# Encoder block on one core: the rotary stage in two passes, and attention's first steps in another order

## The chip, the cores and the metric

The kernel runs on one core of a Trainium2 chip. The metric is device time in microseconds (us) of one execution. The engines are TensorE (PE; its weight loads are PEld), VectorE (DVE), ScalarE (ACT), GpSimd (POOL) and SyncE (SP). Each takes its instructions in order. In this stage SP and POOL only issue DMAs.

## The reference

One encoder block on a sequence of 1024 tokens of width 1024 in float32. One input projection gives the inputs of a Hyena mixer, queries, keys, values and the gates of the two branches. What the change touches is the attention branch between the projection and the softmax, and the point where Hyena's output meets it:

```python
z = h @ w_in[l] + b_in[l]
z_hy, q, k, v, z_g = jnp.split(z, split_at, axis=-1)
...
def rms_norm(x, g):
    xf = x.astype(F32)
    y = xf * lax.rsqrt(jnp.mean(xf * xf, axis=-1, keepdims=True) + EPS)
    return (y * g.astype(F32)).astype(x.dtype)
...
def rot(u, c, s):
    u1, u2 = u[..., :quarter], u[..., quarter:]
    return jnp.concatenate([u1 * c - u2 * s, u1 * s + u2 * c], axis=-1)
...
q = (apply_axial_rope(rms_norm(q, q_gain).astype(F32), cos, sin) * (HEAD_DIM ** -0.5)).astype(v.dtype)
k = apply_axial_rope(rms_norm(k, k_gain).astype(F32), cos, sin).astype(v.dtype)
...
s = jnp.einsum('bkgqd,bksd->bkgqs', qblk, k).astype(F32)
p = jax.nn.softmax(s, axis=-1).astype(v.dtype)
return jnp.einsum('bkgqs,bksd->bkgqd', p, v)
...
g_hy, g_at = jnp.split(jax.nn.sigmoid(z_g), N_BRANCHES, axis=-1)
x = x + gt1 * ((g_hy * y_hy + g_at * y_at) @ w_out[l])
```

There are 8 query heads and 2 key heads of 64 channels. After this stage come the output projection, a router and sixteen experts with their own weights.

## The kernel before

Matrix products are made from float32 values split in a high part (a cast on ScalarE, line L140) and a low part (a difference on VectorE, L141), with three matmuls for each product: L145, L146 and L147 of `mm3`. The block runs as a sequence of stages; a scheduler sets the order of each engine's instructions from the priority under which the code issues them and from dependencies.

**The rotary stage.** The projected queries, keys and values lie in DRAM as `zq_s`, six blocks of 128 channels by 1024 tokens: blocks 0 to 3 are the queries (two heads each), block 4 the keys, block 5 the values. `by_token(b)` loads a block into a tile `X` on SP (L673; two buffers) and turns it to tokens by rows with eight transposes on TensorE (L677). `rotated(b, i)` copies them (ScalarE, L684), squares them (ScalarE, L687), sums each head (VectorE, L689), makes the reciprocal root (`rsqrt`: the square root on ScalarE, L151, then one Newton step in five small VectorE operations, L155 to L159), scales (L692), and rotates (L694, four of L700, L701, all VectorE). `by_channel` turns the result back (TensorE, L707). The keys are cast and stored as four tiles (L724 to L730), the queries as `QT` (high half ScalarE L739, low half VectorE L740, store L742). So each block is one chain through DMA, TensorE, ScalarE, VectorE, TensorE, ScalarE, VectorE, DMA, and each has its own square root.

**The gates.** The sixteen blocks m = 18 to 33 of the projection, `win_block` with the sigmoid of L749 as evacuation, are written last but issued at the priority of the stage's start, so that their matmuls (`pM<-hT,wh` and `pM<-hT,wl`) fill TensorE while the rotary chains run. The sigmoid and the square root use different function tables of ScalarE: a row ACT_TABLE_LOAD stands ahead of each switch.

**Attention.** Its tiles take SBUF addresses that the stage before has used, so their loads on the POOL queue wait for the last user of the address: the first queries (`QT`, L773), two key tiles (`KT`, L783), the values (`Vhl`, L788). Scores of 128 queries are four matmuls (L808, L809) into one of two score buffers `pS`; VectorE takes the row maximum (L814) and ScalarE the exponential with its sum (L816), which frees the score buffer. P is turned on TensorE (L825), split (`ph` L829, `pl` L830) and multiplied by the values (L843, L844).

**Hyena's output beside it.** `hyena_out` loads Hyena's result in eight quarters (`yq`, L871, SP), splits it (`yh`, ScalarE L873; `yl`, VectorE L874), and multiplies it by `why_d` (L885) a few matmuls at a time among attention's. `adaln` (L164, L166, VectorE) adds up one row of weights of the conditioning for each of its eight steps.

## Time and profile before

| what | value |
|---|---|
| time, median of 3 runs | 2242.86 us (2242.12 to 2244.29) |
| time of the profiled execution | 2241.07 us |
| its span in the trace | 2239.3 us |
| mean granted clock of TensorE | 0.98 |
| TensorE busy | 2114.6 us, 94% of the span |
| VectorE busy | 1883.8 us, 84% |
| ScalarE busy | 1313.4 us, 59% |
| DMA | 605.38 MB, 270 GB/s over the span |

The busy shares are averages over stages that have different limits. The profiled execution has 1.8 us around its span. The granted clock is that of TensorE's throttle: 1.0 is its upper level, 2.4 GHz, and 0.5 its lower, 1.2 GHz.

### The profile page before, as it was taken

How to read it: one execution, taken by the hardware profiler on the slowest of the kernel's cores; microseconds unless marked ns; L12 is line 12 of the kernel's file. 1: busy time of each engine (PE TensorE's matmuls, PEld its weight loads, DVE VectorE, ACT ScalarE, POOL GpSimd, SP SyncE). 2: the span in 40 equal slices, each digit the busy share in tenths (PEclk: the TensorE clock that was granted, in tenths of full speed). 3: DMA queues.
4: the chain of work that ended last, by engine and by line, in shares of the span. 5: the costliest groups of instructions: out<-in, count | busy, mean ns of one | idle time of the engine just before them, and what ended most of it. 6: DMA issues, size and time to landing. Idle time of an engine off the chain costs nothing. (4 is left out here: it accounts for less than half of the span.)

```text
span 2239.3 us, 26998 instructions
## 1 busy us (share of the span) xinstructions
PE 2114.6 (94%) x10090; PEld 1683.9 (75%) x10090; DVE 1883.8 (84%) x2132; ACT 1313.4 (59%) x1445; POOL 99.5 (4%) x124
## 2 busy tenths in 40 slices
PE   5899999999589999997899999999999999999997
PEld 2677788887478887774687777777778777787876
DVE  8658899997689888644898899898998989889986
ACT  4933324325477664214577667767776767677674
POOL 0011000000000000001000000000000000000000
PEclk9999999999889999998899999999999999999999
DMA  7568755446533224666699999999999999999995
GB/s 307 195 201 263 239 174 166 145 146 216 191 114 112 78 75 145 230 227 232 260 362 355 340 374 357 367 370 370 374 354 373 368 372 366 357 371 373 379 334 185
DMA packets 157190, 605.38 MB, mean 270 GB/s; under 512 B 14466, under 2 KB 51586, under 8 KB 107780
## 3 DMA queue, kind: packets, MB, share of 16 engines
q1 hardware_dynamic: 141364, 562.77, 67.3%
q0 software_dynamic: 15696, 40.90, 7.0%
q8 instruction: 79, 1.29, 0.2%
q14 instruction: 51, 0.42, 0.1%
HBM read 538.60 MB, written 65.01 MB: 270 GB/s over the span
## 5 line engine op out<-in xcount | busy, mean ns | idle before, releaser
L1227 DVE TENSOR_TENSOR el<-raw,eh 128x2048 fp32r<-128x2048 f32 (+1 forms) x469 | 867.4, 1889 | 48.6 <-ACT eh L1226 45.6
L1226 ACT CAST eh<-raw 128x2048 fp32r<-128x2048 f32 (+1 forms) x471 | 721.0, 1594 | 22.9 <-PE pM L147 10.8
L146 PE MATMUL pM<-el,xh 128*128 128x512 f32 x1024 | 405.3, 396 | 8.2 <-DVE el L1227 7.9
L145 PE MATMUL pM<-eh,xh 128*128 128x512 f32 x1024 | 406.1, 397 | 6.9 <-ACT eh L1226 6.8
L147 PE MATMUL pM<-eh,xl 128*128 128x512 f32 x1024 | 401.5, 392 | 2.6 <-DVE xl L1287 2.6
L146 PEld LDWEIGHTS pM<-el,xh 128*128 128x128 f32 x1024 | 192.7, 188 | 62.1 <-DVE el L1227 25.6
L145 PEld LDWEIGHTS pM<-eh,xh 128*128 128x128 f32 x1024 | 192.5, 188 | 50.1 <-ACT eh L1226 10.0
L147 PEld LDWEIGHTS pM<-eh,xl 128*128 128x128 f32 x1024 | 192.7, 188 | 40.9 <-DVE xl L1287 3.1
L145 PE MATMUL pM<-hT,wh 128*128 128x512 f32 x544 | 214.2, 396 | 7.7 <-ACT z L429 5.1
L147 PE MATMUL pM<-hT,wl 128*128 128x512 f32 x544 | 214.3, 394 | 0.0
L146 PE MATMUL pM<-hT,wh 128*128 128x512 f32 x544 | 214.3, 394 | 0.0
L146 PE MATMUL py<-el,hh 128*128 128x512 f32 x512 | 205.6, 401 | 1.4 <-DVE el L1227 1.3
L145 PE MATMUL py<-eh,hh 128*128 128x512 f32 x512 | 200.8, 392 | 0.4 <-ACT hh L1329 0.4
L147 PE MATMUL py<-eh,hl 128*128 128x512 f32 x512 | 200.0, 391 | 0.3 <-DVE hl L1330 0.2
L140 ACT CAST wh<-wr 128x1024 fp32r<-128x1024 f32 (+1 forms) x58 | 54.0, 932 | 162.1 <-PE pM L146 87.4
L145 PEld LDWEIGHTS pM<-hT,wh 128*128 128x128 f32 x544 | 102.7, 189 | 29.7 <-ACT z L429 5.6
L1317 ACT ACTIVATE hd<-pM 128x512 f32<-128x512 f32 x64 | 38.4, 599 | 142.2 <-PE pM L147 142.2
L146 PEld LDWEIGHTS pM<-hT,wh 128*128 128x128 f32 x544 | 102.9, 189 | 21.1 <-DVE hT L373 0.4
L147 PEld LDWEIGHTS pM<-hT,wl 128*128 128x128 f32 x544 | 102.8, 189 | 20.7
L146 PEld LDWEIGHTS py<-el,hh 128*128 128x128 f32 x512 | 96.1, 188 | 24.6 <-DVE el L1227 5.4
L145 PEld LDWEIGHTS py<-eh,hh 128*128 128x128 f32 x512 | 96.1, 188 | 22.3 <-ACT hh L1329 1.8
L147 PEld LDWEIGHTS py<-eh,hl 128*128 128x128 f32 x512 | 96.3, 188 | 19.3 <-DVE hl L1330 0.9
(380 smaller groups left out, 3399.0 us busy)
## 6 DMA issues: line engine op xcount, KB each, us to landing
raw<-in_wg_dram SPq DMA_DIRECT2D x128, 1024.0 KB, 7.2
raw<-in_wu_dram SPq DMA_DIRECT2D x128, 1024.0 KB, 7.2
raw<-in_wd_dram SPq DMA_DIRECT2D x128, 1024.0 KB, 7.7
wr<-in_win_dram SPq DMA_DIRECT2D x34, 512.0 KB, 4.1
dc<-in_dfc_dram POOLq DMA_DIRECT2D x48, 256.0 KB, 3.7
wr<-in_wada_dram SPq DMA_DIRECT2D x24, 512.0 KB, 3.7
st<-in_wada_dram SPq DMA_DIRECT2D x16, 512.0 KB, 10.0
k_s<-f SPq DMA_DIRECT2D x16, 512.0 KB, 2.8
```

The costliest lines, as they stand in the source:

```text
L140: nc.scalar.copy(h, raw)
L145: mm(o, a[0], b[0], start=start, stop=False)
L146: mm(o, a[0], b[1], start=False, stop=False)
L147: mm(o, a[1], b[0], start=False, stop=stop)
L1226: nc.scalar.copy(h[:, ks], raw[:, ks])
L1227: low = eng.tensor_sub(l[:, ks], raw[:, ks], h[:, ks])
L1317: nc.scalar.activation(hd, ps2[0], AF.Silu)
```

## The change

It has three parts.

First, the rotary stage is in two passes. `by_heads` does the loads, transposes, copies, squares and sums of all five blocks, one after the other; a single Newton chain with one square root then works on all their sums ([128 x 80] instead of five times [128 x 16]); and `rotated` does the rest, block by block. The loads (`load_z`) are issued two blocks ahead. The squares and the rotation's products lie in tiles of another pool (`zt`), the rotated block in the buffers of `X`, which are free by then.

Second, attention: the casts and differences of Hyena's output stand behind the fourth exponential and the fifth maximum (`behind` orders instructions of one engine without a semaphore), and the rows of `adaln` behind the sixth maximum.

Third, the first P tile is taken early from its pool, so that it, and not the first queries' tile, lies on the addresses which are used last in the rotary stage.

The lines of after.py are numbered a little higher than those of before: L147 becomes L152, L677 L688, L684 L700, L687 L702, L707 L724, L739 L767, L808 L838, L816 L846, L873 L903.

```diff
@@ -129,6 +129,11 @@
         tc.add_manual_dep(late.ins, early.ins.name, mybir.DependencyInfo(
             mybir.DependencyClass.Sync, mybir.DependencyReason.DATA), reason="wait")
 
+    def behind(late, early):
+
+        tc.add_manual_dep(late.ins, early.ins.name, mybir.DependencyInfo(
+            mybir.DependencyClass.NoSync, mybir.DependencyReason.DATA), reason="behind")
+
     def wload(src, cols_=1024):
         t = ring.tile([128, cols_], F32, name="wr", tag="wr", bufs=2)
         nc.sync.dma_start(t, src)
@@ -161,9 +166,9 @@
     def adaln(acc, w, k):
 
         if k == 0:
-            nc.vector.tensor_scalar(acc, w, siluc[:, 0:1], None, op0=ALU.mult)
+            return nc.vector.tensor_scalar(acc, w, siluc[:, 0:1], None, op0=ALU.mult)
         else:
-            nc.vector.scalar_tensor_tensor(acc, w, siluc[:, k:k + 1], acc, op0=ALU.mult, op1=ALU.add)
+            return nc.vector.scalar_tensor_tensor(acc, w, siluc[:, k:k + 1], acc, op0=ALU.mult, op1=ALU.add)
 
     def mod_cols(acc, g, psum):
         ps = psum([128, 8])
@@ -658,7 +663,7 @@
         tabs = []
         for i in range(2):
             g = gain[:, i]
-            tab = f4([128, 2, 8, 64])
+            tab = w2("H", [128, 2, 8, 64])
             nc.vector.tensor_mul(tab[:, 0], rope[:, 0], g[:, None, :].to_broadcast([128, 8, 64]))
             for u in range(2):
                 for h in range(2):
@@ -668,9 +673,15 @@
                                          g[:, None, i_].to_broadcast([128, 8, 16]))
             tabs.append(tab)
 
+        zs = {}
+
+        def load_z(b):
+
+            zs[b] = w2("X", [128, 1024])
+            nc.sync.dma_start(zs[b], zq_s[b])
+
         def by_token(b):
-            z = w2("X", [128, 1024])
-            nc.sync.dma_start(z, zq_s[b])
+            z = zs[b]
             for hf in range(2):
                 ps = pT()
                 for j in range(4):
@@ -678,27 +689,33 @@
                                         z[:, (hf * 4 + j) * 128:(hf * 4 + j + 1) * 128], ident)
                 yield hf, ps.rearrange("p (q c) -> p q c", q=4)
 
-        def rotated(b, i):
-            tok = f4([128, 8, 2, 64])
+        blocks = (4, 0, 1, 2, 3)
+        ms = w2("wf").rearrange("p (i n) -> p i n", i=4)[:, 0:3, 0:80]
+        toks = {}
+
+        def by_heads(n, b):
+
+            tok = toks[b] = f4([128, 8, 2, 64])
             for hf, ps in by_token(b):
                 nc.scalar.copy(tok[:, hf * 4:hf * 4 + 4].rearrange("p q h c -> p q (h c)"), ps)
+            sq = zt().rearrange("p (n c) -> p n c", n=16)
+            nc.scalar.activation(sq, tok.rearrange("p q h c -> p (q h) c"), AF.Square)
+            nc.vector.reduce_sum(ms[:, 0, n * 16:n * 16 + 16], sq, axis=AX.X)
+
+        def rotated(n, b, i):
+            tok = toks.pop(b)
             t2 = tok.rearrange("p q h c -> p (q h) c")
-            sq = f4([128, 16, 64])
-            nc.scalar.activation(sq, t2, AF.Square)
-            m = w2("ms", [128, 3, 16])
-            nc.vector.reduce_sum(m[:, 0], sq, axis=AX.X)
-            nc.vector.tensor_scalar(m[:, 0], m[:, 0], 1.0 / 64, EPS, op0=ALU.mult, op1=ALU.add)
-            rsqrt(m[:, 1], m[:, 0], m[:, 2])
-            nc.vector.tensor_mul(t2, t2, m[:, 1][:, :, None].to_broadcast([128, 16, 64]))
-            A = f4([128, 8, 2, 64])
+            nc.vector.tensor_mul(t2, t2, ms[:, 1, n * 16:n * 16 + 16][:, :, None].to_broadcast([128, 16, 64]))
+            A = w2("X", [128, 8, 2, 64])
             nc.vector.tensor_mul(A, tok, tabs[i][:, 0][:, :, None, :].to_broadcast([128, 8, 2, 64]))
+            turn = zt().rearrange("p (q h c) -> p q h c", q=8, h=2)
             for h in range(2):
                 src = tok[:, :, h].rearrange("p q (a u c) -> p q a u c", a=2, u=2)
-                dst = sq.rearrange("p (q h) c -> p q h c", h=2)[:, :, h].rearrange("p q (a u c) -> p q a u c", a=2, u=2)
+                dst = turn[:, :, h].rearrange("p q (a u c) -> p q a u c", a=2, u=2)
                 tab = tabs[i][:, 1].rearrange("p q (a u c) -> p q a u c", a=2, u=2)
                 for u in range(2):
                     nc.vector.tensor_mul(dst[:, :, :, u], src[:, :, :, 1 - u], tab[:, :, :, u])
-            nc.vector.tensor_add(A, A, sq.rearrange("p (q h) c -> p q h c", h=2))
+            nc.vector.tensor_add(A, A, turn)
             return A
 
         def by_channel(R, hf):
@@ -708,15 +725,26 @@
                                     R[:, hf * 4 + j].rearrange("p h c -> p (h c)"), ident)
             return ps
 
-        Vhl = f4([128, 2, 4, 2, 64], F32R), f4([128, 2, 4, 2, 64], F32R)
+        load_z(5)
+        load_z(4)
+        Vhl = [z4([128, 2, 4, 2, 64], F32R) for hf in range(2)]
         for hf, ps in by_token(5):
-            p4 = ps.rearrange("p q (h c) -> p h q c", h=2)
+            if hf:
+                load_z(0)
+            p4 = ps.rearrange("p q (h c) -> p h q c", c=64)
             nc.scalar.copy(Vhl[hf][:, :, :, 0], p4)
             nc.vector.tensor_sub(Vhl[hf][:, :, :, 1], p4, Vhl[hf][:, :, :, 0])
+        for n, b in enumerate(blocks):
+            by_heads(n, b)
+            if n < 3:
+                load_z(blocks[n + 2])
+        for hf in range(2):
             nc.sync.dma_start(V_s[:, hf], Vhl[hf].rearrange("p h q s c -> p (h q s c)").bitcast(F32))
+        nc.vector.tensor_scalar(ms[:, 0], ms[:, 0], 1.0 / 64, EPS, op0=ALU.mult, op1=ALU.add)
+        rsqrt(ms[:, 1], ms[:, 0], ms[:, 2])
         lo, hi = slice(0, 64), slice(64, 128)
         K = [[f4([128, 1024], F32R) for h in range(2)] for i in range(2)]
-        R = rotated(4, 1)
+        R = rotated(0, 4, 1)
         for hf in range(2):
             sl = slice(hf * 512, hf * 512 + 512)
             ps = by_channel(R, hf)
@@ -730,7 +758,7 @@
                 nc.sync.dma_start(KT_s[i, h], K[i][h].bitcast(F32))
 
         for b_ in range(4):
-            R = rotated(b_, 0)
+            R = rotated(b_ + 1, b_, 0)
             QT = [wk.tile([128, 1024], F32R, name="QT", tag="Z", bufs=4) for h in range(2)]
             for hf in range(2):
                 sl = slice(hf * 512, hf * 512 + 512)
@@ -768,6 +796,8 @@
         def w(name, shape, dt=F32, bufs=2):
             return at.tile(list(shape), dt, name=name, tag=name, bufs=bufs)
 
+        firstP = w("P", [128, 1024], bufs=6)
+
         def query(h):
             t = w("QT", [128, 1024], F32R)
             return t, nc.gpsimd.dma_start(t, QT_s[h])
@@ -776,7 +806,7 @@
         KT = [[w(f"KT{i}{h}", [128, 1024], F32R, 1) for h in range(2)] for i in range(2)]
         Vhl = w("Vhl", [128, 2, 2, 4, 128], F32R, 1)
 
-        exps = []
+        exps, maxima = [], []
 
         def keys(kv):
             for i in range(2):
@@ -811,8 +841,8 @@
                         yield
                 Sf = S.rearrange("p n k -> p (n k)")
                 c = (i % 2) * 2 + j
-                nc.vector.tensor_reduce(rs[:, c:c + 1], Sf, axis=AX.X, op=ALU.max, negate=True)
-                P = w("P", [128, 1024], bufs=6)
+                maxima.append(nc.vector.tensor_reduce(rs[:, c:c + 1], Sf, axis=AX.X, op=ALU.max, negate=True))
+                P = w("P", [128, 1024], bufs=6) if exps else firstP
                 exps.append(nc.scalar.activation(P, Sf, AF.Exp, bias=rs[:, c:c + 1], accum_out=rs[:, 4 + c:5 + c]))
                 Ps.append(P)
                 yield
@@ -870,8 +900,8 @@
                 t = yp.tile([128, 4, 128], F32, name="yq", tag="yq", bufs=2)
                 nc.sync.dma_start(t, y_s[q])
                 sl = slice(q * 128, q * 128 + 128)
-                nc.scalar.copy(yh[:, :, sl], t)
-                nc.vector.tensor_sub(yl[:, :, sl], t, yh[:, :, sl])
+                behind(nc.scalar.copy(yh[:, :, sl], t), exps[3])
+                behind(nc.vector.tensor_sub(yl[:, :, sl], t, yh[:, :, sl]), maxima[4])
             acc = yp.tile([128, 1024], F32, name="acc")
             for m in range(8):
                 raw = wload(why_d[m], 512)
@@ -890,7 +920,7 @@
                     nc.vector.tensor_mul(g, ps, g)
                     nc.sync.dma_start(m1_s[m][:, sl], g)
                     yield
-                adaln(acc, wload(wada_d[2, m]), m)
+                behind(adaln(acc, wload(wada_d[2, m]), m), maxima[5])
             mod_cols(acc, 2, pT)
 
         units = [(h, i) for h in range(8) for i in range(4)]
```

On TensorE, among the gate matmuls behind the transposes of the values and keys, the order before has only gate matmuls for more than fifty rows. In the change, the transposes of blocks 0 to 3 (L688) stand there; these are the rows around those of blocks 1 and 2:

```order
L151 MATMUL pM<-hT_340,wh 128x512
L152 MATMUL pM<-hT_332,wl 128x512
L150 MATMUL pM<-hT_333,wh 128x512
L688 MATMUL pT<-ident,X 128x128 x8
L151 MATMUL pM<-hT_341,wh 128x512
L152 MATMUL pM<-hT_333,wl 128x512
L688 MATMUL pT<-ident,X 128x128 x8
L150 MATMUL pM<-hT_334,wh 128x512
L151 MATMUL pM<-hT_342,wh 128x512
L152 MATMUL pM<-hT_334,wl 128x512
```

Two gate matmuls lie between block 1 and block 2. Block 0 stands ten gate matmuls ahead of block 1, and block 3 fourteen behind block 2.

The end of the gates on TensorE before (L146, L147 are gate matmuls; L707 are the transposes of blocks 2 and 3, rotated; L677 those of block 3's z; L808 and L809 the first scores):

```order
L145 MATMUL pM<-hT_338,wh 128x512
L146 MATMUL pM<-hT_346,wh 128x512
L147 MATMUL pM<-hT_338,wl 128x512
L707 MATMUL pT<-ident,f_3736 128x128 x8
L677 MATMUL pT<-ident,X 128x128 x8
L707 MATMUL pT<-ident,f_3792 128x128 x8
L808 MATMUL pS<-KT_4835,QT 128x512 x2
L809 MATMUL pS<-KT_4837,QT 128x512
```

and in the change (L151, L152 the gates, L724 the rotated block 3, L838 and L839 the scores):

```order
L150 MATMUL pM<-hT_338,wh 128x512
L151 MATMUL pM<-hT_346,wh 128x512
L152 MATMUL pM<-hT_338,wl 128x512
L724 MATMUL pT<-ident,X 128x128 x8
L838 MATMUL pS<-KT_4809,QT 128x512 x2
L839 MATMUL pS<-KT_4811,QT 128x512
L838 MATMUL pS<-KT_4809,QT 128x512
```

Behind the last gate matmul one group of eight transposes is left of three.

On ScalarE, the end of the rotary stage and attention's start before: the last two blocks' casts (L739), copies, square and square root of block 3 (L684, L687, L151), the casts of Hyena's output (L873), the exponentials (L816) and the high parts of P (L829):

```order
L739 CAST QT<-pT 64x512 x4
L684 COPY f_3765<-pT 128x512 x2
L687 ACTIVATE f_3780<-f_3765 128x1024
L151 ACT_TABLE_LOAD
L151 ACTIVATE ms<-ms 128x16
L739 CAST QT<-pT 64x512 x4
L873 CAST yh<-yq 128x4x128 x4
L816 ACT_TABLE_LOAD
L816 ACTIVATE P,rs<-pS,rs 128x1024 x2
L873 CAST yh<-yq 128x4x128 x2
L829 CAST ph<-pM 128x512 x2
```

and in the change (L767 the casts, L777 the sigmoid of a gate, L846 the exponentials, L859 the high parts, L903 Hyena's casts):

```order
L777 ACTIVATE ge<-pM,cols 128x512
L767 CAST QT<-pT 64x512 x4
L846 ACT_TABLE_LOAD
L846 ACTIVATE P,rs<-pS,rs 128x1024 x2
L859 CAST ph<-pM 128x512
L846 ACTIVATE P,rs<-pS,rs 128x1024
L859 CAST ph<-pM 128x512 x2
L846 ACTIVATE P,rs<-pS,rs 128x1024
L903 CAST yh<-yq 128x4x128
L859 CAST ph<-pM 128x512
L903 CAST yh<-yq 128x4x128
```

The exponentials' table load stands right behind the last block's casts, four exponentials precede the first cast of Hyena's output, and no square root is left there.

## Rows read from the trace of the kernel before

**Rows 1.** The page, part 2: busy tenths of DMA in 40 slices

```profile
DMA  7568755446533224666699999999999999999995
```

**Rows 2.** Windows: length, busy by engine, granted PE clock, DMA share, GB/s

```profile
521.00:584.00 63.00, 62.12 (x303) 49.92 (x302) 42.53 (x78) 39.68 (x55) 0.00 (x0) 1.00 0.56 201
584.00:625.50 41.50, 8.65 (x34) 6.27 (x33) 25.65 (x40) 14.83 (x24) 2.12 (x4) 0.63 0.59 212
625.50:680.00 54.50, 54.44 (x347) 47.70 (x348) 48.88 (x67) 40.92 (x73) 2.12 (x4) 0.97 0.30 100
```

**Rows 3.** Timeline of TensorE: start, us, operation, count, [idle before <-releaser]

```profile
583.70 0.39 PE L147 MATMUL pM<-hT,wl 128*128 128x512 f32 x1
589.82 1.94 PE L707 MATMUL pT<-ident,f 128*128 128x128 f32 x8 [5.73 <-DVE f L701]
...
605.65 1.94 PE L707 MATMUL pT<-ident,f 128*128 128x128 f32 x8 [9.80 <-DVE f L701]
...
609.91 0.50 PE L809 MATMUL pS<-KT,QT 128*128 128x512 f32 x1 [1.22 <-DMA KT<-KT_s]
...
625.49 0.79 PE L808 MATMUL pS<-KT,QT 128*128 128x512 f32 x1 [13.95 <-ACT P L816]
```

**Rows 4.** Timeline of ScalarE in the same stretch

```profile
616.03 1.36 ACT L873 CAST yh<-yq 128x512 fp32r<-128x512 f32 x2 [6.49 <-DMA yq<-y_s]
...
622.23 1.28 ACT L816 ACT_TABLE_LOAD   x1
```

**Rows 5.** Timeline of VectorE in the same stretch

```profile
610.30 0.75 DVE L164 TENSOR_SCALAR acc<-wr,siluc 128x1024 f32<-128x1024 f32 x1
611.09 1.28 DVE L166 SCALAR_TENSOR_TENSOR acc<-wr,siluc,acc 128x1024 f32<-128x1024 f32 x1
...
622.97 2.35 DVE L814 TENSOR_REDUCE rs<-pS 128x1 f32<-128x1024 f32 x2
```

**Rows 6.** Timeline of POOL: issues of attention's first loads

```profile
602.25 0.53 POOL L773 DMA_DIRECT2D QT<-QT_s  x1 [95.81 <-DVE f L692]
602.77 1.07 POOL L783 DMA_DIRECT2D KT<-KT_s  x2
```

**Rows 7.** Timeline of SP: issues of the loads of blocks 0 and 1

```profile
523.24 0.32 SPq L673 DMA_DIRECT2D X<-zq_s  x1
...
525.35 0.52 SPq L673 DMA_DIRECT2D X<-zq_s  x1
```

**Rows 8.** Tile X, in 523.2:523.3 and in 525.2:525.5: landing in us

```profile
DMA to landing us min/median/max: 5.2/5.2/5.2
...
DMA to landing us min/median/max: 7.3/7.3/7.3
```

**Rows 9.** Timeline of TensorE among the gate matmuls

```profile
524.72 0.60 PE L677 MATMUL pT<-ident,X 128*128 128x128 f32 x4
525.07 0.48 PE L147 MATMUL pM<-hT,wl 128*128 128x512 f32 x1
...
536.98 0.39 PE L145 MATMUL pM<-hT,wh 128*128 128x512 f32 x1
```

**Rows 10.** Timeline of VectorE: block 3's rotation, first and last, low halves

```profile
600.43 1.22 DVE L692 TENSOR_TENSOR f<-f,ms 128x1024 f32<-128x1024 f32 x1
...
604.28 1.22 DVE L701 TENSOR_TENSOR f<-f,f 128x1024 f32<-128x1024 f32 x1
...
608.24 2.02 DVE L740 TENSOR_TENSOR QT<-pT,QT 64x512 fp32r<-64x512 f32 x3 [0.17 <-ACT QT L739]
```

**Rows 11.** Timeline of TensorE in a later stage, a wait for VectorE

```profile
894.86 0.50 PE L145 MATMUL pS<-oT,wh 128*128 128x512 f32 x1 [1.60 <-DVE g L947]
```

**Rows 12.** Windows, right behind that wait

```profile
897.00:898.80 1.80, 1.80 (x5) 1.35 (x5) 0.68 (x2) 0.00 (x0) 0.00 (x0) 0.50 0.95 327
```

**Rows 13.** Lines, 521 to 626 us: loads of ScalarE's tables

```profile
L151 ACT ACT_TABLE_LOAD x5 | 6.4, 1283 | 0.1
...
L749 ACT ACT_TABLE_LOAD x4 | 5.1, 1283 | 0.1
```

## The prediction

> **What bounds the kernel now.** The page's DMA slices [rows 1] stand at nine tenths only in the second half of the span, where the experts' weights are read; the rotary stage lies near slice 10, where DMA is no limit. So I read the stretches around it [rows 2]. From 521 to 584 us TensorE is busy 62.12 of 63 us: gate matmuls bound it. From 584 to 625.5 it is busy 8.65 of 41.5, at a mean granted clock of 0.63. From 625.5 on attention keeps it busy 54.44 of 54.5, with DVE at 48.88. The hole between the two full stretches is the stage to read.
>
> TensorE's timeline there [rows 3]: the last gate matmul starts at 583.70 and ends at 584.09; the transposes of block 2's rotated queries wait 5.73 for DVE, those of block 3's 9.80; scores start, wait 1.22 for a key tile, and go on from 609.91 until both score buffers are full. Then TensorE waits 13.95 for the first exponential, until 625.49. That last wait is explained on ScalarE [rows 4]: it stands at 616.03 in a cast of Hyena's output that waited 6.49 for a DMA, and loads the exponential's table only at 622.23. On VectorE [rows 5] two adaLN rows, then the low halves of the casts, stand ahead of the first maximum, which starts at 622.97 although the matmuls of its scores began at 609.91 at the latest. The loads of attention's first tiles sat on the POOL queue until 602.25 behind a wait of 95.81 on the last block's norm [rows 6]. So 584.09 to 625.49, 41.40 us, is one chain: two blocks' rotary work one after the other, loads, then a queue of casts.
>
> **Term 1: the gates end later.** All five blocks' z transposes now stand among the first sixty gate matmuls, so TensorE, which works in order, waits in the gates where z isn't there. The loads of blocks 0 and 1 go out at 523.24 and 525.35 [rows 7], when blocks 5 and 4 are transposed; this order hasn't changed. They landed after 5.2 and 7.3 us [rows 8], at 528.4 and 532.65. Gate matmuls come every 0.229 us (52 of them from 525.07 to 536.98 [rows 9]). Block 0's transposes stand seven gate matmuls behind 525.07, so at 526.7: a wait of 1.8. Eight transposes take about 0.85. Ten gate matmuls on, at 531.6, block 1: a wait of 1.05. The load of block 2 starts when block 0 is transposed, at 529.4; landing in 5.6, an estimate nearer to the shorter of the two, it is there at 535.0, and TensorE two gate matmuls behind block 1 at 533.9: 1.1. Block 3's load starts at 533.5, lands at 539.1, and TensorE comes there at 539.0: 0.1. Sum 4.05; with landings at 5.2 throughout about 3, at 7.3 about 7.
>
> Two groups of eight transposes that stood behind the gates (block 3's z, block 2's rotated queries [rows 3]) now lie ahead of the last gate matmul: 2 x 0.85 = 1.7. The 0.85 is an estimate: four transposes at 524.72 held the next matmul off for 0.35 [rows 9], twice that is 0.70, and the matmuls around them start a little late. The 1.94 for eight in [rows 3], behind a long wait, bounds it from above. Will a rotated block be late for its transposes? A rotation takes DVE from 600.43 to 605.50, 5.07 us, and the low halves of its casts 2.02 for three of four [rows 10], 2.7 in all; with about 1 us for a weight's low half that is 8.8 per block, against 36 to 40 gate matmuls and eight transposes, 9.1 to 10.0, on TensorE. DVE just keeps up; I take 0.5 in sum, bounds 0 and 3. The norms' own chain, five squares and sums and one square root, ends near 548 and its first block is due near 556: covered by 65 gate matmuls (14.9 us); without that cover it would cost its 3 to 4 us.
>
> The clock: behind a wait of 1.60 at 894.86 [rows 11] the granted clock is 0.50, which is 1.2 GHz, up to 898.8, and five matmuls stand there in 1.8 us [rows 12] where eight would at 0.229. From 894.86 to 898.8 are 3.9 us; at half speed they lose up to 2.0, and I count 1.6 for a drop. Block 0's wait of 1.8 is of that size; most of what it costs is taken from the next two waits, since those end when a load lands. I take 1.0, bounds 0 and 4.8 (three drops). [...]
>
> Term 1 is 4.05 + 1.7 + 0.5 + 1.0 = 7.25: gates end near 591.35 instead of 584.09.
>
> **Term 2: from the gates' end to the first exponential.** The queries' tile leaves the address range whose last user was block 3's norm. By the order of the new code, its load waits for one of the last gate matmuls, and the first key load for the very last. So they go out at 591.4. Meanwhile block 3, rotated near 593, is transposed (1.94 in [rows 3]) and cast, and ScalarE loads the exponential's table (1.28 [rows 4]); with four casts of some 0.6 that is done by 597, ahead of the first maximum near 599.5. From the first key load's issue (602.77 [rows 6]) to the matmul that used the last key tile (609.91) it took 7.14; the first block of scores needs about 1.0 more; from the first maximum's start (622.97) to TensorE's restart it took 2.52. Sum 10.7: restart at 602.05, that is 23.4 us earlier than 625.49. Hyena's casts no longer lie between. The bounds of the 7.14: the two landings of [rows 8] lie 2.1 apart, so plus or minus 1.
>
> **Term 3: attention's first part.** What was done in the hole must now be done beside TensorE's work: adaLN's first three rows (0.75 + 2 x 1.28), and Hyena's casts, of which four and their low halves lay in the hole. DVE had 5.6 of 54.5 us free [rows 2]. The new load is some 2.0 for two adaLN rows and 2.8 for four low halves (0.69 each), 4.8 in all, less 1.2 since a third maximum is done before: it fits by a margin of 2. Since queues in order don't fill perfectly I take a loss of 1.5, bounds 0 and 5. Everything behind 680 keeps its order and shifts.
>
> **Sum.** 7.25 + 10.7 = 17.95 for 41.40, less 1.5: 21.95 us gained. The profiled execution took 2241.07 us (span 2239.3); it would become 2219.1. The median of the runs shown is 1.79 above it, so the forecast is 2220.9. Differences under 0.2% (4.5 us) can't be told from no change.
>
> **The rivals.**
> A: the norm pass holds TensorE longer. Landings of 7.3 (7 instead of 4.05) and three clock drops (4.8 instead of 1.0) make term 1 14.0; restart 6.75 later: 2227.7. For it: DMA is busy there, with stores of V and gate outputs beside the loads; against it: a slower TensorE arrives later at the next load.
> B: VectorE becomes the bound in early attention, by the 88 to 90% that it is already busy [rows 2]: loss 5 to 6 instead of 1.5, 2225.4. Against it: the low halves wait behind the fifth maximum, and the first use of them comes late.
> C: only the table loads count, because some other wait holds the scores where they were. Five loads for square roots and four back to the sigmoid [rows 13] become one and one: 7 x 1.283 = 9.0, so 2233.9. The Trainium skill, "ScalarE: Activation LUTs", section "What ACT_TABLE_LOAD costs", puts a switch at about 2.66 us with a drain; by that figure this case alone would be 18.6 us, an estimate. Here the load is 1.283 and nothing in the rows shows a drain of that size.
> D: no change: the gain is given back in the experts' stage, where DMA is at nine tenths [rows 1]. Against it: its buffers come free with the work ahead, so its stream shifts too. 2242.9.
> E: slower: the gate matmuls stand in order behind the z transposes. Block 3's load starts when block 1 is transposed, so when landings T are long, block 3's transposes come at about 527.9 + 2T (539.1 at 5.6, term 1), and 193 gate matmuls and the key loads stand behind them. The gain of 21.95 is gone when 2T has grown by as much, at T of 16.6, and from there every us of landing costs two: at T of 20 it would be 2249.7. Against it: of the two landings shown the longer is 7.3 [rows 8]. For it: all four loads fall into a stretch in which stores of V and of gate outputs are due.
>
> **How the numbers follow.** Forecast 0.70, with its own range 2215.9 to 2227.8 (below, all terms at their low bounds: waits -1.05, clock -1.0, rotations -0.5, keys -1, attention -1.5, together 5.05; above, half of what the upper bounds add: waits 2.95, clock 3.8, rotations 2.5, keys 1, attention 3.5, together 13.75). A 0.12, B 0.07, C 0.04, D 0.03, E 0.04. The range for 8 in 10 is 2215 to 2231: A and B and three quarters of the sum of the upper bounds lie below its upper end, C, D and E above it. Faster: 0.70 + 0.12 + 0.07 + 0.04 = 0.93; same 0.03; slower 0.04.
>
> **What would show it.** Right: four short waits of TensorE for X between 526 and 541; the last gate matmul near 591; one table load for the root, one back; key loads on POOL within 1 us of the last gate matmul; first exponential ending near 602, with no Hyena cast ahead of it; attention's end near 836 instead of 858. Wrong: gates ending after 596; waits of TensorE for rotated blocks of over 1 us each; the key load waiting for something else; TensorE waiting for `pl` or for `yl` in the first 50 us of attention; a longer gap between attention and experts than before.

## The result and the profile after

The changed kernel takes 2217.76 us (median of 4 runs, 2216.80 to 2220.59) against 2242.49 for the kernel before (4 runs): the ratio is 0.9893, with a 95% interval of 0.9876 to 0.991. That is 24.7 us less, where 21.95 were forecast. The profiled execution took 2217.21 us with a span of 2215.4, that is 23.9 under the one of before.

The windows of the changed kernel, with the columns of [rows 2]:

```profile
521.00:591.00 70.00, 64.17 (x319) 51.58 (x317) 53.28 (x78) 37.81 (x57) 2.12 (x4) 1.00 0.55 197
591.00:602.00 11.00, 6.36 (x14) 4.06 (x15) 4.73 (x7) 4.88 (x8) 0.54 (x1) 0.52 1.05 390
602.00:657.00 55.00, 53.68 (x343) 46.31 (x342) 51.54 (x72) 41.42 (x75) 1.59 (x3) 0.97 0.44 144
```

The windows are cut where the forecast put the gates' end (591.35); the gates themselves end at 587.78. From there to TensorE's restart it takes 11.99 us, where it took 41.40, and the gates' stretch is 4.70 longer (table below). From 591 to 602 the DMA engines have a share of 1.05 and move 390 GB/s; the granted clock is 0.52 there and 1.00 up to 591.

TensorE's timeline answers to [rows 3]:

```profile
528.15 1.06 PE L688 MATMUL pT<-ident,X 128*128 128x128 f32 x8 [1.54 <-DMA X<-zq_s]
...
533.84 1.06 PE L688 MATMUL pT<-ident,X 128*128 128x128 f32 x8 [0.98 <-DMA X<-zq_s]
...
564.23 1.06 PE L724 MATMUL pT<-ident,X 128*128 128x128 f32 x8 [0.50 <-DVE X L718]
...
573.00 1.06 PE L724 MATMUL pT<-ident,X 128*128 128x128 f32 x8 [0.20 <-DVE X L718]
...
587.39 0.39 PE L152 MATMUL pM<-hT,wl 128*128 128x512 f32 x1
589.26 1.06 PE L724 MATMUL pT<-ident,X 128*128 128x128 f32 x8 [1.48 <-DVE X L718]
593.78 1.19 PE L838 MATMUL pS<-KT,QT 128*128 128x512 f32 x2 [3.46 <-DMA KT<-KT_s]
595.57 0.80 PE L839 MATMUL pS<-KT,QT 128*128 128x512 f32 x1 [0.59 <-DMA KT<-KT_s]
...
599.77 0.79 PE L838 MATMUL pS<-KT,QT 128*128 128x512 f32 x1 [1.27 <-ACT P L846]
```

Two z loads are waited for, 1.54 and 0.98; two rotated blocks, 0.50 and 0.20; the last gate matmul starts at 587.39. Of the three groups of transposes behind it one is left, with a wait of 1.48. Then the key tiles are waited for, 3.46 and 0.59, and the wait for the first exponential is 1.27 where it was 13.95. TensorE restarts at 599.77 instead of 625.49.

ScalarE, VectorE and POOL answer to [rows 4 to 6]:

```profile
592.49 1.28 ACT L846 ACT_TABLE_LOAD   x1
598.51 1.11 ACT L846 ACTIVATE P<-pS,rs 128x1024 f32<-128x1024 f32 x1 [4.74 <-DVE rs L844]
```

```profile
590.58 2.63 DVE L768 TENSOR_TENSOR QT<-pT,QT 64x512 fp32r<-64x512 f32 x4 [0.86 <-ACT QT L767]
597.25 2.50 DVE L844 TENSOR_REDUCE rs<-pS 128x1 f32<-128x1024 f32 x2 [4.04 <-PE pS L839]
```

```profile
587.40 0.53 POOL L803 DMA_DIRECT2D QT<-QT_s  x1 [81.96 <-DMA QT_s<-QT]
588.08 1.06 POOL L813 DMA_DIRECT2D KT<-KT_s  x2
```

Neither a cast of Hyena's output nor an adaLN row stands between block 3's last casts and the first maximum; ScalarE waits 4.74 and VectorE 4.04 for scores, which wait for the key loads, and these go out right behind the last gate matmul.

The span can be cut at five starts that every kernel here has: block 5's first transposes, the last gate matmul, the first exponential, the last matmul with V, the first expert matmul. All are read from the timelines. The first exponential of the kernel before, which [rows 4] do not show, is this row:

```profile
624.23 1.11 ACT L816 ACTIVATE P<-pS,rs 128x1024 f32<-128x1024 f32 x1 [0.71 <-DVE rs L814]
```

| stretch | before | changed | difference |
|---|---|---|---|
| up to block 5's transposes | 521.42 | 520.41 | -1.01 |
| to the last gate matmul | 62.28 | 66.98 | +4.70 |
| to the first exponential | 40.53 | 11.12 | -29.41 |
| to attention's last matmul with V | 242.04 | 244.40 | +2.36 |
| to the first expert matmul | 212.90 | 212.23 | -0.67 |
| to the end | 1160.13 | 1160.26 | +0.13 |

The first row isn't the change's: the difference is there already at VectorE's first instruction that is not the same, a row of the rotation's table (517.50 before, 516.49 in the changed kernel), and over the other traces of this study the row goes from 520.20 to 524.56. So a profiled span is read here by its stretches. The experts' stage keeps its length to 0.13: nothing is given back there.

### The profile page after: what moved, and what is told of

Its sections match the earlier page's. It is cut to its first block, busy times and chain, and to the rows that moved or that the text cites. A ratio compares the mean times of both kernels' runs of the same rounds, so it can differ in the third digit from the quotient of the medians.

```text
span 2215.4 us, 26961 instructions
## 1 busy us (share of the span) xinstructions
PE 2113.6 (95%) x10090; PEld 1681.6 (76%) x10090; DVE 1878.2 (85%) x2108; ACT 1301.8 (59%) x1434; POOL 99.5 (4%) x124
## 5 line engine op out<-in xcount | busy, mean ns | idle before, releaser
L1256 ACT CAST eh<-raw 128x2048 fp32r<-128x2048 f32 (+1 forms) x471 | 720.9, 1594 | 23.1 <-PE pM L152 10.7
L151 PE MATMUL pM<-el,xh 128*128 128x512 f32 x1024 | 405.3, 396 | 8.1 <-DVE el L1257 7.9
L152 PE MATMUL pM<-eh,xl 128*128 128x512 f32 x1024 | 401.8, 393 | 2.7 <-DVE xl L1317 2.7
L151 PEld LDWEIGHTS pM<-el,xh 128*128 128x128 f32 x1024 | 192.7, 188 | 62.3 <-DVE el L1257 25.1
L152 PEld LDWEIGHTS pM<-eh,xl 128*128 128x128 f32 x1024 | 192.7, 188 | 40.8 <-DVE xl L1317 3.2
L152 PE MATMUL pM<-hT,wl 128*128 128x512 f32 x544 | 214.2, 394 | 0.0
L151 PE MATMUL pM<-hT,wh 128*128 128x512 f32 x544 | 214.1, 394 | 0.0
L151 PE MATMUL py<-el,hh 128*128 128x512 f32 x512 | 205.6, 402 | 1.4 <-DVE el L1257 1.3
L152 PE MATMUL py<-eh,hl 128*128 128x512 f32 x512 | 200.1, 391 | 0.3 <-DVE hl L1360 0.2
L151 PEld LDWEIGHTS pM<-hT,wh 128*128 128x128 f32 x544 | 102.9, 189 | 20.9 <-DVE hT L378 0.6
L152 PEld LDWEIGHTS pM<-hT,wl 128*128 128x128 f32 x544 | 102.8, 189 | 20.8
L151 PEld LDWEIGHTS py<-el,hh 128*128 128x128 f32 x512 | 96.1, 188 | 24.6 <-DVE el L1257 5.4
L152 PEld LDWEIGHTS py<-eh,hl 128*128 128x128 f32 x512 | 96.3, 188 | 19.3 <-DVE hl L1360 0.9
```

The source lines that it names most:

```text
L151: mm(o, a[0], b[1], start=False, stop=False)
L152: mm(o, a[1], b[0], start=False, stop=stop)
L1256: nc.scalar.copy(h[:, ks], raw[:, ks])
```

## Experiments

### Each half alone

The first kernel has the new rotary stage only, the second the new order of attention's start only.

```diff
 # two passes only
-        firstP = w("P", [128, 1024], bufs=6)
...
-                behind(nc.scalar.copy(yh[:, :, sl], t), exps[3])
-                behind(nc.vector.tensor_sub(yl[:, :, sl], t, yh[:, :, sl]), maxima[4])
+                nc.scalar.copy(yh[:, :, sl], t)
+                nc.vector.tensor_sub(yl[:, :, sl], t, yh[:, :, sl])
...
-                behind(adaln(acc, wload(wada_d[2, m]), m), maxima[5])
+                adaln(acc, wload(wada_d[2, m]), m)
```

> Only the rotary stage is changed (two passes, one root). Hyena's casts and the adaLN rows stand ahead of the first exponential as before, and the first P tile is taken where it was. If the casts ahead of the exponential are worth what their place in the old chain says, the first four casts end near 604, the exponential's table is loaded near 605, and TensorE restarts near 608 instead of 599.8 in the changed kernel; about 2 us come back in early attention, which then has less to do: 2224, some 18 under the kernel before. Rival: the loads for Hyena's casts start so much earlier that the casts are done before the scores anyway: then it equals the changed kernel, 2217.8.

> Only the order of attention's start is changed; the rotary stage is that of before. Scores start at 609.9 as before; the first maximum should follow near 611 instead of 622.97 and TensorE restart near 613.6 instead of 625.49, 11.9 earlier; early attention gives back about 2: 2232.8, some 9.7 under before. Rival: it gains all of 11.9 or more (what is lost in early attention then comes from something else than the moved casts), 2230.6; or nothing, if the casts only move the wait.

Two passes alone: 2232.38 us, ratio 0.9957 (0.9941 to 0.9974). The order alone: 2228.27 us, ratio 0.9944 (0.9926 to 0.9962). Both moved the way that was expected; the first is 8 us slower than I expected and the second 4.5 faster. (The first kernel's profiled execution was the quickest of its four, 2228.51, so its stretches flatter it.) ScalarE with two passes only:

```profile
602.50 0.62 ACT L901 CAST yh<-yq 128x512 fp32r<-128x512 f32 x1 [9.06 <-DMA yq<-y_s]
...
608.51 0.62 ACT L901 CAST yh<-yq 128x512 fp32r<-128x512 f32 x1 [1.47 <-DMA yq<-y_s]
609.14 1.28 ACT L844 ACT_TABLE_LOAD   x1
611.14 1.11 ACT L844 ACTIVATE P<-pS,rs 128x1024 f32<-128x1024 f32 x1 [0.71 <-DVE rs L842]
```

The last gate matmul starts at 587.99 there and the first exponential 23.15 later, against 11.12 in the changed kernel and 40.53 before. The casts wait 9.06 for Hyena's loads, since these go out behind the last queries' store and land in the full DMA queue (410 GB/s from 593.5 to 602.5): I had taken 604 for the fourth cast, it ends at 609.13. The order alone leaves the gates where they were (62.25 us) and brings the first exponential to 27.86 behind the last gate matmul, 12.67 sooner than before:

```profile
606.66 1.94 PE L712 MATMUL pT<-ident,f 128*128 128x128 f32 x8 [9.81 <-DVE f L706]
...
613.82 0.50 PE L813 MATMUL pS<-KT,QT 128*128 128x512 f32 x1 [2.41 <-ACT P L821]
```

The wait of 9.81 for block 3's rotation is as in [rows 3], and the one for the first exponential falls from 13.95 to 2.41. From the first exponential to attention's end it takes 242.10, against 242.04 before: the 2 us that I expected early attention to give back did not come, which was the rival of that expectation. Against the 2241.83 of the kernel before, measured beside them, the two halves are worth 9.5 and 13.6 us, 23.0 in sum, and the whole change 24.7: they take different parts of one chain.

### Which of the moved work held the scores

```diff
-                behind(adaln(acc, wload(wada_d[2, m]), m), maxima[5])
+                adaln(acc, wload(wada_d[2, m]), m)
```

> The changed kernel with adaLN's rows free to be placed as before: three rows then stand ahead of the first maximum on VectorE (0.75 + 2 x 1.28 = 3.3 us). VectorE has 4.04 us idle there in the changed kernel. Theory A: the rows wait for their weights (the first load is issued at 589.7 and takes 5, the next two follow in a ring of two buffers that Hyena's output weights share), so the first exponential comes 3 to 8 us later and most of it is lost: 2220 to 2225. Theory B: they fit into the idle time, the first exponential moves by under 1, and early attention gains the 3.3 us of VectorE: 2216 to 2217.

2233.55 us, ratio 0.9957 (0.9941 to 0.9974): theory A, and more than it said. VectorE:

```profile
598.27 0.75 DVE L169 TENSOR_SCALAR acc<-wr,siluc 128x1024 f32<-128x1024 f32 x1
604.78 1.28 DVE L171 SCALAR_TENSOR_TENSOR acc<-wr,siluc,acc 128x1024 f32<-128x1024 f32 x1 [5.76 <-DMA wr<-in_wada_dram]
611.74 1.29 DVE L171 SCALAR_TENSOR_TENSOR acc<-wr,siluc,acc 128x1024 f32<-128x1024 f32 x1 [5.67 <-DMA wr<-in_wada_dram]
613.05 2.36 DVE L844 TENSOR_REDUCE rs<-pS 128x1 f32<-128x1024 f32 x2
```

Each of the second and third rows waits nearly 6 us for its weights, and the first maximum stands behind them in order. The first exponential comes 21.88 behind the last gate matmul, close to the 23.15 of the kernel with two passes only, in which the casts stand ahead of it, with two adaLN rows, and the third part of the change is missing. So there are two queues side by side, ScalarE's casts and VectorE's adaLN rows, and either one can hold the scores. Moving the casts and not the rows brings the first exponential 1.3 us sooner, and no shorter time (2233.55 against 2232.38). Moving the rows and not the casts was not tried.

### One root, or five

```diff
             nc.vector.reduce_sum(ms[:, 0, n * 16:n * 16 + 16], sq, axis=AX.X)
+            m = ms[:, :, n * 16:n * 16 + 16]
+            nc.vector.tensor_scalar(m[:, 0], m[:, 0], 1.0 / 64, EPS, op0=ALU.mult, op1=ALU.add)
+            rsqrt(m[:, 1], m[:, 0], m[:, 2])
...
-        nc.vector.tensor_scalar(ms[:, 0], ms[:, 0], 1.0 / 64, EPS, op0=ALU.mult, op1=ALU.add)
-        rsqrt(ms[:, 1], ms[:, 0], ms[:, 2])
```

> The changed kernel with a square root and Newton chain for each block in the first pass, so eight table loads more on ScalarE, 10.3 us. My theory: they lie beside the gate matmuls and cost 0 to 3, say 1: 2218.8. Rival: one root is what the gain is made of, and it costs 8 to 10: 2226 to 2228.

2221.83 us, ratio 0.9911 (0.9894 to 0.9927); the interval overlaps the changed kernel's. The table loads are there (lines view, 521 to 600 us):

```profile
L156 ACT ACT_TABLE_LOAD x5 | 6.4, 1283 | 0.1
L778 ACT ACT_TABLE_LOAD x5 | 6.4, 1283 | 0.1
```

These are ten where the changed kernel has two, 10.3 us more on ScalarE, and the gates end 67.51 behind block 5 instead of 66.98: 0.5 (block 3's rotated transposes stand four gate matmuls ahead of the last one there, and not behind it). Another 1.6 stands between gates and first exponential, where the key tiles landed after 7.0 and 8.5 instead of 6.9. So the number of roots is not what the gain is made of. That the norms of all blocks being ready before the rotations makes it is argued from the order; no kernel here takes that away alone.

### Where the loads wait

Three kernels vary the loads between gates and scores: without the early P tile; with V's load behind the first maximum; and with attention's pools in another order, so that the first loads no longer wait for the gates.

```diff
 # loads off the gates' addresses
+        opool = right.enter_context(tc.tile_pool(name="op", bufs=1, side="right", reuse_waits="tile"))
         at = right.enter_context(tc.tile_pool(name="at", bufs=1, side="right", reuse_waits="tile"))
...
-        firstP = w("P", [128, 1024], bufs=6)
-        KT = [[w(f"KT{i}{h}", [128, 1024], F32R, 1) for h in range(2)] for i in range(2)]
+        KT = [[w("KT00", [128, 1024], F32R, 1), w("KT01", [128, 1024], F32R, 1)]]
+        late = w("KT11", [128, 1024], F32R, 1)
+        KT.append([w("KT10", [128, 1024], F32R, 1), late])
 # V late
-        nc.gpsimd.dma_start(Vhl.rearrange("p f h q c -> p f (h q c)"), V_s)
+                if len(exps) == 1:
+                    load = nc.gpsimd.dma_start(Vhl.rearrange("p f h q c -> p f (h q c)"), V_s)
+                    wait(load, maxima[0])
```

> The changed kernel without its third part: the first P tile is taken when it is first written. By the addresses, the queries' load then waits for the first and not the seventh of the last gate group's eight tiles, and the key loads for the third and fifth instead of the last. My theory: key loads go out 3 to 4 us earlier, scores start right behind block 3's transposes near 590.4 instead of 593.8, restart of TensorE 3 us earlier: 2214.8. Rival: the third part is needed, the queries' tile waits for something later than the gates and the restart comes later: 2219 or more.

> The changed kernel with the load of V (1 MB) put behind the first maximum, so that it isn't in flight beside the queries' and keys' tiles. My theory: the stretch from the gates' end to the first maximum is bound by DMA bandwidth (390 GB/s at a share of 1.0 from 588 to 600), so without V the last key tile lands about 1.5 us sooner after its issue (6.0 instead of 7.5) and the first exponential comes 1 to 1.5 us sooner behind the last gate matmul (10 instead of 11.1); V itself lands near 605, when its first matmul is due, and may cost 0 to 2 there: 2216 to 2219, no difference in the time. Rival: a fixed landing time of some 7 us whatever else is in flight; then the exponential stays at 11.1 and the kernel loses what V's landing adds, 2219 to 2221.

> The changed kernel with attention's tiles laid out otherwise (the output tiles' pool first, then the queries, the keys of the first half, V; the first P tile where it is first written): by the addresses, the first loads of queries, keys and V no longer wait for any gate matmul, only for their own stores and for users that end before 535. My theory: they go out before 580, are there when the gates end, TensorE goes from block 3's transposes to the scores without a wait near 590.4, the first maximum follows block 3's last low half near 593.3, the first exponential near 594.4 instead of 598.5, TensorE restarts near 595.6, and its clock is back sooner: 4 to 5 us under the changed kernel, 2213. Rival: the restart is bound by block 3's own chain (casts, table load) and by DMA for other tiles, and it gains 0 to 2: 2216 to 2218.

Without the early P tile: 2219.53 us, ratio 0.9898 (0.9882 to 0.9915), which can't be told from the changed kernel. The key loads do go out sooner, 2.5 and 1.1 us ahead of the last gate matmul at 589.73 instead of 0.7 and more behind it:

```profile
587.22 0.53 POOL L811 DMA_DIRECT2D KT<-KT_s  x1 [2.02 <-PE pM L152]
588.59 0.53 POOL L811 DMA_DIRECT2D KT<-KT_s  x1 [0.84 <-ACT QT L767]
```

But they land 7.4 and 8.2 us after their issue instead of 6.9, and the first exponential comes 10.04 behind the last gate matmul instead of 11.12: 1.1 of the 3 that I expected. The restart, at 601.03, finds the clock back at its upper level:

```profile
601.00:606.20 5.20, 5.13 (x29) 4.14 (x30) 3.91 (x6) 4.31 (x8) 0.53 (x1) 1.00 1.06 412
```

From the first exponential to attention's end it takes 242.49 here, 1.9 less than in the changed kernel, and attention ends 2.6 us sooner behind block 5. The next stretch, to the experts, is 2.1 longer (214.37). Whether the third part gains or costs anything can't be told from these times.

With V late: 2222.81 us, ratio 0.9912 (0.9895 to 0.9928). From 588 to 600 the DMA engines move 331 GB/s, against 356 in the changed kernel (not 390, as the expectation has it). The keys land after 5.8 and 7.2, at best a little sooner, and the first exponential stays at 11.35 behind the gates. V takes 8.3 us and is then waited for:

```profile
609.85 0.55 PE L875 MATMUL pT<-ph,Vhl 128*128 128x256 f32 x1 [2.76 <-DMA Vhl<-V_s]
```

So the landing of the keys is not V's doing alone. What else is in flight there are stores of queries and the loads for Hyena's output; that these are enough was not tested. The expectation for V's own landing (605) was too early.

With the loads off the gates' addresses:

```profile
572.43 0.53 POOL L801 DMA_DIRECT2D QT<-QT_s  x1 [66.02 <-DVE zt L717]
572.95 1.07 POOL L813 DMA_DIRECT2D KT<-KT_s  x2
```

```profile
590.79 1.06 PE L724 MATMUL pT<-ident,X 128*128 128x128 f32 x8 [1.48 <-DVE X L718]
591.61 0.71 PE L838 MATMUL pS<-KT,QT 128*128 128x512 f32 x2
...
597.30 0.80 PE L838 MATMUL pS<-KT,QT 128*128 128x512 f32 x1 [3.60 <-ACT P L846]
```

The queries' load now waits for a rotation product (`zt`) on VectorE, and the keys go out behind it, 16 us ahead of the gates' end; they land after 5.6 to 6.3, and the scores follow block 3's transposes without a wait. The first exponential comes 7.11 behind the last gate matmul, 4.0 sooner than in the changed kernel, as expected. Yet the time is 2218.15 us, ratio 0.989 (0.9874 to 0.9907), the same as the changed kernel's. The stretches say where it went: 245.20 instead of 244.40 to attention's end, 213.95 instead of 212.23 to the experts, 1162.01 instead of 1160.26 to the end. Attention still ends 2.6 us sooner behind block 5 than in the changed kernel. The stretch to the experts varies from 211.80 to 214.37 us over the kernels of this study, so its 1.72 tells nothing. The last stretch is 1160.04 to 1160.74 in all the others, also in the kernel below that has these same loads with the idle time filled, so the layout is not the cause of its 1.75. In this trace alone the clock falls once among the experts:

```profile
1227.60:1231.00 3.40, 3.40 (x8) 2.72 (x9) 3.40 (x3) 3.40 (x3) 0.00 (x0) 0.50 1.01 402
```

Half of 3.4 us is 1.7, which accounts for the 1.75. The wait ahead of that drop is on the experts' weights' casts (0.96 at 1226.89), far from the loads that this kernel moves.

### What early attention loses

TensorE's clock behind the restart, in the changed kernel:

```profile
528.10:532.00 3.90, 3.85 (x24) 3.40 (x25) 0.99 (x1) 2.71 (x4) 0.00 (x0) 1.00 0.59 174
599.70:604.90 5.20, 5.13 (x16) 4.25 (x17) 1.97 (x3) 3.17 (x7) 0.54 (x1) 0.50 1.06 404
605.00:609.90 4.90, 4.90 (x35) 4.25 (x34) 4.58 (x7) 3.86 (x8) 0.00 (x0) 1.00 0.51 181
```

For 5.2 us behind the restart the clock is at 0.50. Two kernels fill TensorE's wait with 32 transposes of a tile that is there, into a PSUM tile that nobody reads: the changed kernel behind block 3's transposes, and the kernel with the loads off the gates' addresses behind its first eight score matmuls.

```diff
+        idle = pM()
+        for n in range(32):
+            nc.tensor.transpose(idle[:, n % 4 * 128:n % 4 * 128 + 128], R[:, n % 8].rearrange("p h c -> p (h c)"), ident)
```

> The changed kernel with 32 more transposes of block 3's rotated tile on TensorE behind block 3's own, into a score-sized PSUM tile that nobody reads: work without use, which fills the wait for the key tiles (3.46 us in the changed kernel, 32 at about 0.1). Theory clock: what early attention lost there (244.4 us from the first exponential to attention's end against 242.0 before) is the lowered clock behind that wait, 0.50 for the 5.2 us behind the restart; with TensorE kept busy the scores run at 1.0, the first exponential comes about 1 us sooner behind the last gate matmul (10.1 instead of 11.1) and the stretch from it to attention's end is 242 to 242.5: 2214.6. Theory casts: the loss is Hyena's casts and adaLN beside the exponentials; then the stretch stays at 244 to 245 and the time at 2217 to 2218.

> The kernel with the loads off the gates' addresses, and 32 transposes of a key tile that nobody reads behind the first eight score matmuls, to fill the 3.60 us wait for the first exponential. Theory clock: the stretch from the first exponential to attention's end falls from 245.2 to about 242.5, since the restart is at full clock, and the kernel from 2218.2 to 2215.6. Theory casts: no difference.

In the changed kernel the filling moved the wait instead of taking it away: the scores run at full clock, the first exponential comes 10.09 behind the last gate matmul as expected, but then TensorE waits 1.86 for it, and behind that wait the clock falls after all:

```profile
591.45 3.66 PE L783 MATMUL pM<-ident,X 128*128 128x128 f32 x32
...
600.05 0.70 PE L841 MATMUL pS<-KT,QT 128*128 128x512 f32 x1 [1.86 <-ACT P L849]
```

```profile
600.20:603.60 3.40, 3.40 (x11) 2.77 (x12) 1.22 (x1) 1.40 (x3) 0.53 (x1) 0.50 1.02 411
```

From the first exponential to attention's end it took 243.90 instead of 244.40, and the time is 2218.94 us, ratio 0.99 (0.9883 to 0.9916): no gain. In the other kernel no wait is left:

```profile
593.20:597.00 3.80, 3.69 (x34) 3.43 (x32) 3.59 (x4) 3.05 (x5) 0.00 (x0) 1.00 0.98 365
597.00:602.60 5.60, 5.52 (x33) 4.54 (x34) 4.31 (x6) 4.62 (x8) 0.53 (x1) 1.00 0.99 346
```

The clock stays at 1.00, the stretch is 243.49 instead of 245.20, and the time 2216.03 us, ratio 0.9885 (0.9868 to 0.9901), 2.1 under its own base where 2.6 were expected. It is the quickest kernel here, but its interval overlaps those of its base and of the changed kernel. So in these traces the clock at the restart is worth 1.7 us of attention; the kernel without the early P tile, with its clock up and 1.9 less, agrees. The difference of the times is not clear of the noise. It can't be all of the 2.36 that attention lost, since the kernel before restarts at a lowered clock as well.

The last kernel leaves out the low halves of Hyena's output.

```diff
-                behind(nc.vector.tensor_sub(yl[:, :, sl], t, yh[:, :, sl]), maxima[4])
...
-                        for i, (a, b) in enumerate(((wh, yh), (wh, yl), (wl, yh))):
+                        for i, (a, b) in enumerate(((wh, yh), (wh, yh), (wl, yh))):
```

> The changed kernel without the low halves of Hyena's output (eight differences of 0.69 on VectorE left out; the matmuls that used them read the high halves, as many as before). Theory: what early attention still loses beside the clock is VectorE's share of the moved casts: the stretch from the first exponential to attention's end falls from 244.4 to 242 to 243 and the time to 2216. Rival: it is ScalarE's casts, or the order on TensorE; then it stays at 244 and 2217.8.

2218.55 us, ratio 0.9893 (0.9877 to 0.991), and 245.20 in the stretch: no gain, so VectorE's 5.5 us of low halves don't set it alone. TensorE waits 1.07 for a cast there:

```profile
614.09 0.74 PE L913 MATMUL pT<-yh,wh 128*128 128x512 f32 x2 [1.07 <-ACT yh L902]
```

## Why the prediction was right

**Term 1**, gates later by 7.25: measured 4.70. The waits for z are two, of 2.52 in sum, in place of four of 4.05. Block 0's load ended TensorE's wait 5.9 us after its issue; those of blocks 1 to 3 landed in 4.5 to 5.5 us, where 7.3 and 5.6 were taken, and block 1, with 1.05 forecast, was not waited for. One of the two V stores, which had been in flight beside block 1's load, goes out later now. The waits for rotated blocks are 0.70 (0.5 forecast). With 1.7 for the two groups of transposes that makes 4.9. The clock term, 1.0, measured nothing in this execution: behind the wait of 1.54 the granted clock is 1.00 (528.1 to 532.0 above). It wasn't without reason, though. In the kernel with V late, whose rotary stage is the same, the wait for block 0 happened to be 2.21, and there it fell:

```profile
526.00:530.10 4.10, 1.94 (x10) 1.29 (x8) 1.22 (x1) 1.65 (x2) 0.00 (x0) 1.00 0.93 290
530.10:534.00 3.90, 3.85 (x15) 3.30 (x16) 0.87 (x1) 2.81 (x4) 0.00 (x0) 0.60 0.64 185
```

The next z wait, 0.98 in the changed kernel, was gone there, as the prediction argued: the later loads take part of a drop up. Its net cost can't be read here: the gates ended 67.62 behind block 5, and 66.76 to 67.87 in the kernels with the same rotary stage and no drop. In the kernel with adaLN's rows free the same wait was 2.25, and the clock stayed up:

```profile
532.30 1.06 PE L688 MATMUL pT<-ident,X 128*128 128x128 f32 x8 [2.25 <-DMA X<-zq_s]
```

```profile
532.30:536.20 3.90, 3.90 (x25) 3.42 (x26) 1.03 (x1) 2.76 (x5) 0.00 (x0) 1.00 0.72 175
```

So the length of a wait alone does not say whether the clock falls. The wait of 1.60 in [rows 11], on which this term was priced, says the same: it is 1.41 in the changed kernel and 1.58 with two passes only, and the clock stays at 1.00 behind both. The drop of the kernel before, worth up to 1.7 us, lies in its stretch from attention to the experts; that the change took it away isn't shown.

**Term 2**, 10.7 from the gates' end to TensorE's restart: measured 11.99, from 587.78 to 599.77. From the first key load's issue to the matmul that used the last key tile it took 7.49 (7.14 forecast), and from there to the first maximum 1.68 (1.0), since the scores run at the lowered clock behind the wait for the keys: this I had not counted. From the first maximum to the restart it took 2.52, as forecast. Block 3's chain ended at 593.77 with the table load, well ahead.

**Term 3**, 1.5: measured 2.36 in attention. Of the 2.36, 1.24 are two waits of TensorE that the kernel before does not have:

```profile
612.84 0.39 PE L874 MATMUL pT<-pl,Vhl 128*128 128x256 f32 x1 [0.76 <-DVE pl L860]
...
627.14 0.50 PE L838 MATMUL pS<-KT,QT 128*128 128x512 f32 x1 [0.48 <-ACT P L846]
```

About 0.8 more come from the clock: it is low for 5.2 us behind the restart against 3.6 before, and half of the 1.6 is lost:

```profile
625.50:629.10 3.60, 3.60 (x11) 2.81 (x12) 3.01 (x4) 2.69 (x5) 0.54 (x1) 0.50 0.75 241
```

The rest, 0.3, is open. The kernel with the order alone has the two waits as well (0.76 and 0.42) but the full clock at its restart, and loses nothing (242.10). So the clock, which this term did not hold, is a good part of the loss. My reason, that VectorE has little room, fits the first wait: two low halves and a maximum stand on VectorE ahead of that `pl`.

```profile
609.56 1.26 DVE L904 TENSOR_TENSOR yl<-yq,yh 128x512 fp32r<-128x512 f32 x2
...
612.10 1.28 DVE L860 TENSOR_TENSOR pl<-pM,ph 128x512 fp32r<-128x512 f32 x2
```

Without the low halves both waits are gone, but the stretch is no shorter, and a wait of 1.07 for a cast stands in their place. A wait for `pl` in the first 50 us was one of the prediction's signs of being wrong; it came, and cost 0.76.

Together: 4.70 - 29.41 + 2.36 - 0.67 + 0.13 = -22.9 from block 5's transposes on, and -1.0 that lay ahead of them. The forecast was 21.95. The mechanism and its places were right: most of the last two blocks' rotary work went beside the gates, and the scores no longer wait for casts and rows. The largest mis-sized item is the waits for z, 1.5 too long. That the sum came so near is partly luck: term 1 was 2.55 too long, terms 2 and 3 were 1.3 and 0.9 too short. The prediction's 858 for attention's end before is not the last matmul with V, which starts at 866.27; that one moved by 23.4 us, where 22 were forecast.

**The rivals.** A did not come: no landing of 7.3, and a drop among the gates in one of the ten kernels with two passes. B did not: the loss is 2.4, not 5 to 6. C is refuted by the five roots, which cost 0 to 4 with eight loads of 1.283 more: the loads lie beside the gates. D did not come, with the experts' stage at +0.13. E's condition, 16.6 us of landing, is far from the 4.5 to 5.9 measured. Its sum is a little off: the 527.9 holds block 1's landing of 7.3; with one T for both loads it is 525.35 + 0.85 + 2T, and the condition 17.4.

## What to carry over

When a stage ends in a wait, look on every engine that feeds the next step for work that stands in order ahead of it and is not needed by it: here two queues, casts on ScalarE and adaLN rows on VectorE, held the same scores, and moving the casts alone brought the first exponential 1.3 us sooner, both together 12. A chain that is run once per block costs its length only for the blocks that have nothing beside them; doing all blocks' first halves early put the last two under the gate matmuls, and the number of square roots hardly mattered. And a start that is brought forward need not show in the time: of the 4.0 us that the loads off the gates' addresses gave the first exponential, 2.6 were left at attention's end, and none in the kernel's time.

## What the hardware did that I had not expected

Loads issued sooner landed only about 1 us sooner, while the DMA engines were full. In the changed kernel (356 GB/s from 588 to 600) the second key tile, 512 KB, landed 6.9 us after its issue, 8.1 behind the last gate matmul. Issued some 2 to 3 us sooner, without the early P tile, the two tiles landed after 7.4 and 8.2, the second 7.1 behind the last gate matmul. Issued at 573, with the loads off the gates' addresses, they landed after 5.6 and 6.3, though the DMA engines moved 360 GB/s there too (572 to 580, a share of 1.04).

A wait of TensorE of 2.21 us was followed by a granted clock of 0.50, 1.2 GHz; one of 2.25, in the same place of another kernel, was not, and one of 1.60 [rows 11] was.
